# A decoder's MLP in eight blocks of 512 inner features, its second product as seven block products summed in DRAM

## The chip, the cores and the metric

The kernel runs on one core of a Trainium2 chip. Such a core has TensorE (PE, with its weight loads PEld), VectorE (DVE), ScalarE (ACT), GpSimd (POOL), SyncE (SP, which here only issues DMAs) and 16 DMA engines. Each engine works through its own queue in order and waits on semaphores for the others. The metric is device time in microseconds of one execution; the median of several runs counts.

## The reference

Two layers of a hybrid decoder on 512 tokens with 1024 features, then a last RMS norm. In each layer a wide projection feeds sliding-window attention and a retention branch, which are gated and added (that half is not touched here), and then comes the MLP:

```
x = x + mixed @ w_out
h2 = rmsnorm(x, g_mlp)
x = x + jnp.square(jax.nn.relu(h2 @ w_up)) @ w_down     # w_up 1024 x 4096, w_down 4096 x 1024
...
return rmsnorm(x, g_final)                               # after both layers
```

Everything is float32. The kernel gets its accuracy from three products of rounded parts: each operand is split into hi (rounded by ScalarE to the matmul's type) and lo (the rest, by VectorE), and hi·hi + hi·lo + lo·hi are summed in PSUM.

## The kernel before

x lies transposed in SBUF: features in partitions (8 chunks of 128), the 512 tokens in columns. A matmul has a 128x128 block of a weight as its stationary operand and 512 (or 256) tokens as the moving one, and its output has features in partitions again.

**Weights** come in units of 128x1024 (512 KB) in one order fixed beforehand (`unit_order`). `load_until` issues the loads on SP's queue into a ring of three raw buffers, `split_until` has ScalarE write hi (L235) and VectorE lo (L236) into rings of three each, and `unit` hands the next pair to the products and asks for the splits up to three units further on. `products` (L280 to L282) issues the three matmuls of each 128x128 block.

**First product of the MLP.** The first 512 inner features are a plain product (`group`, four units, four PSUM banks, `put_up`). The other 3584 come in 14 pairs of two 128-feature chunks (`pair`): a product of two by two blocks made with seven block products in place of eight. For it the weights are added to each other (`load_part`, `add_part`, VectorE), the input's four sums are made once per layer (`sum_input`), PSUM results are copied or added by ScalarE and VectorE (L1037 to L1049), each block product has 256 tokens, 12 matmuls, and relu, the RMS factor and the square follow (L1053, L1054, L1057). The result is split into hi and lo and kept in slots (`Slots`: nine tiles of 128x2048, given out in quarters or whole).

**Second product.** The inner features are taken in four quarters of 1024. `mlp_sequence` writes the order out by hand: the pairs of the next quarter alternate with `two_chunks` of w_down for the quarter before (two output chunks, two units, 48 matmuls of 512 tokens), whose result VectorE adds to x (L1064). The last quarter comes after all pairs: in layer 0 a group of four chunks and four single ones, and as each chunk of x is done the next layer's input is scaled, split, squared and spilled. In layer 1 `end` takes the tokens in two halves of 256, so that the last norm of the first half goes on beside the second half's products; it squares, sums over features with a matmul against ones, takes the root and reciprocal, multiplies and stores.

All instructions are ordered by a scheduler from the order in which the program issues them; on one engine they then run in that order.

Of the kernel before, what the change touches and what calls it, by code (L numbers as in the profile page):

```python
# [17 lines left out]
P = 128  # L18
# [25 lines left out]
N_IN = 46  # L44
UNIT = 1024
# [3 lines left out]
DELAY = 2  # L49


def unit_order():
# [9 lines left out]
    for what, q, i in mlp_sequence():  # L62
        if what == "first":
            order += [("w_up", u) for u in range(4)]
        elif what == "pair":
            order += [("pair", 8 * q + 2 * i, part) for part in range(4)]
        elif what == "down":
            order += [("w_down", 8 * q + 2 * i + u) for u in range(2)]
        else:
            order += [("w_down", 8 * q + u) for u in range(8)]  # L70
    return order


def mlp_sequence():

    seq = [("first", 0, 0), ("pair", 0, 2), ("pair", 0, 3)]
    for q in range(3):
        for i in range(4):  # L80
            seq += [("down", q, i), ("pair", q + 1, i)]
    return seq + [("last", 3, 0)]
# [32 lines left out]
def decoder(ctx, tc, xT, x_first, w_in, w_a, w_b, w_out, w_up, w_down, tables, decay, band, out):  # L115
# [14 lines left out]
    def temp(name="t"):  # L130
        return tmp.tile([P, T], F32, tag="t", name=name)
# [23 lines left out]
    raws, parts, homes = {}, {}, []  # L155
# [6 lines left out]
    def raw_tile():  # L162
        return wpool.tile([P, UNIT], F32, tag="raw", name="raw")

# [7 lines left out]
    def load_until(n):  # L172
        while state["loaded"] < min(n, len(order)):
            i = state["loaded"]
            layer, name, j = order[i][:3]
            if name == "pair":
                load_part(i)
            else:
# [13 lines left out]
    def load_part(i):  # L192
        layer, _, j, part = order[i]
        if part == 0:
            raws[i] = raw_tile()
            nc.sync.dma_start(raws[i][:, LEFT], w_up[layer, j][:, LEFT])
            raws[i + 3] = raw_tile()
            nc.sync.dma_start(raws[i + 3], w_up[layer, j + 1])
        elif part == 1:
            raws[i] = big("raw2").rearrange("p a t -> p (a t)")  # L200
            nc.sync.dma_start(raws[i][:, RIGHT], w_up[layer, j][:, RIGHT])

    def add_part(i):
        part = order[i][3]
        if part == 0:
            w2 = raws[i + 3]
            nc.vector.tensor_tensor(raws[i][:, RIGHT], w2[:, RIGHT], w2[:, LEFT], ALU.add)
        elif part == 1:
            w1 = raws[i - 1]
            nc.vector.tensor_tensor(raws[i][:, LEFT], w1[:, RIGHT], w1[:, LEFT], ALU.subtract)  # L210
        elif part == 2:
            raws[i] = big("raw3").rearrange("p a t -> p (a t)")
            w1, w2, z2 = raws[i - 2], raws[i + 1], raws[i - 1]
            nc.vector.tensor_tensor(raws[i][:, LEFT], w1[:, LEFT], w2[:, RIGHT], ALU.subtract)
            nc.vector.tensor_tensor(raws[i][:, RIGHT], z2[:, RIGHT], z2[:, LEFT], ALU.subtract)

    def split_until(n):
        while state["split"] < min(n, len(order)):
            i = state["split"]
            load_until(i + 3)  # L220
            paired = order[i][1] == "pair"
            if paired:
                add_part(i)
            raw = raws[i]
            if homes and i >= len(order) - len(homes):
                home = homes[len(order) - 1 - i]
                hi, lo = (home[:, 2 * a : 2 * a + 2, :].rearrange("p a t -> p (a t)") for a in range(2))
            else:
                hi = wpool.tile([P, UNIT], F32R, tag="hi", name="hi")
                lo = wpool.tile([P, UNIT], F32R, tag="lo", name="lo")  # L230
# [172 lines left out]
    def end(layer, uT):  # L403
# [5 lines left out]
        def unit_at(i):  # L409
            if len(units) == i:  # L410
                units.append(unit("w_down", layer))
            return units[i]
# [841 lines left out]
```

## Time and profile before

| | |
|---|---|
| median of 3 runs | 1511.3 us (1511.27 to 1512.82) |
| the profiled execution | span 1511.4 us, 20498 instructions |
| PE busy | 99%, 8080 matmuls |
| VectorE, ScalarE, POOL busy | 68%, 49%, 0% |
| HBM read, written | 146.96 MB, 4.19 MB |
| MLP of layer 0, of layer 1 (from the timeline) | about 415 to 753 us, 1160 to 1501 us |

The page has one row for each group of equal instructions: line, engine, operation, output and inputs by the program's names, shapes and count, then busy time and mean of one in ns, then the idle time ahead of them and what ended it. A wait row has engine, line, "<-" what it waited for, total us, times and the longest. A timeline row has start and duration in us.

### The profile page before, as it was taken

Reading aid. Unit: us, or ns where it says so; the run is one execution under the profiler, and the core shown is the slowest. Engines: PE = TensorE matmul, PEld = TensorE weight load, DVE = VectorE, ACT = ScalarE, POOL = GpSimd, SP = SyncE. Lnnn points to the kernel's source line nnn. Section 1 sums busy time; section 2 is a strip of 40 time slices with the busy share of each in tenths; the row PEclk is TensorE's granted clock in tenths of the full one; section 3 lists DMA queues with packets and bytes.
Section 4 is the critical chain, followed back from the end, with each engine's and each line's share of the span. In section 5 each row is a group of like instructions: output and inputs, shape, how many; then the busy total and the mean of one; then the engine's idle time right before and its main releaser. Section 6 shows DMA issues by size and latency. Waiting matters only on the chain.

```text
span 1511.4 us, 20498 instructions
## 1 busy us (share of the span) xinstructions
PE 1499.2 (99%) x8080; PEld 1302.2 (86%) x8080; DVE 1026.7 (68%) x1598; ACT 740.1 (49%) x1163; POOL 2.9 (0%) x13
## 2 busy tenths in 40 slices
PE   9999999999999999999999999999999999999997
PEld 7888888888888999989888888888888999889997
DVE  6877668754787666676678765777449866666664
ACT  6656455632564444444455742555327544444452
POOL 0000000000000000000000000000000000000000
PEclk9999999999999999999999999999999999999999
DMA  6422322233223232233442222222342232232331
GB/s 217 123 97 75 98 79 91 70 125 126 98 78 104 98 112 97 93 104 115 165 131 93 84 84 98 82 79 84 126 125 98 85 104 92 99 111 98 103 108 56
DMA packets 52640, 155.10 MB, mean 103 GB/s; under 512 B 6208, under 2 KB 8384, under 8 KB 52544
## 3 DMA queue, kind: packets, MB, share of 16 engines
q1 hardware_dynamic: 52400, 153.54, 30.6%
q8 instruction: 63, 1.03, 0.3%
q14 instruction: 33, 0.27, 0.1%
q10 hardware_dynamic: 144, 0.26, 0.0%
HBM read 146.96 MB, written 4.19 MB: 100 GB/s over the span
## 4 chain that ended last, share of the span: by engine, by line
PE 98%; ACT 1%; DVE 0%; DMA 0%; issue 0%; DVEq 0%
PE mm L280 29%; PE mm L281 29%; PE mm L282 29%; PE rv L280 2%; PE rv L281 2%; PE rv L282 2%; PE score L651 1%; PE pT L616 1%; PE r L281 1%; PE r L282 1%; PE r L280 1%; PE pv L637 0%; PE pv L636 0%; PE ssq L374 0%; PE ret L281 0%; PE ret L282 0%
## 5 line engine op out<-in xcount | busy, mean ns | idle before, releaser
L235 ACT ACTIVATE hi<-raw 128x1024 fp32r<-128x1024 f32 (+1 forms) x313 | 314.6, 1013 | 517.9 <-PE mm L281 430.6
L236 DVE TENSOR_TENSOR lo<-raw,hi 128x1024 fp32r<-128x1024 f32 (+1 forms) x314 | 362.6, 1164 | 162.0 <-ACT hi L235 161.1
L281 PE MATMUL mm<-r,hi 128*128 128x512 f32 (+1 forms) x1136 | 392.5, 346 | 0.0
L280 PE MATMUL mm<-r,hi 128*128 128x512 f32 (+1 forms) x1136 | 389.5, 346 | 1.0 <-ACT mm L1037 1.0
L282 PE MATMUL mm<-r,lo 128*128 128x512 f32 (+1 forms) x1136 | 388.5, 346 | 0.0
L280 PE MATMUL mm<-xh,hi 128*128 128x512 f32 (+1 forms) x1008 | 358.2, 357 | 0.9 <-ACT xh L290 0.9
L281 PE MATMUL mm<-xl,hi 128*128 128x512 f32 (+1 forms) x1008 | 356.8, 356 | 0.0
L282 PE MATMUL mm<-xh,lo 128*128 128x512 f32 (+1 forms) x1008 | 355.4, 356 | 0.0
L280 PEld LDWEIGHTS mm<-r,hi 128*128 128x128 f32 x1136 | 214.8, 189 | 27.8 <-ACT mm L1037 1.4
L281 PEld LDWEIGHTS mm<-r,hi 128*128 128x128 f32 x1136 | 215.3, 189 | 26.3
L282 PEld LDWEIGHTS mm<-r,lo 128*128 128x128 f32 x1136 | 215.0, 189 | 25.7
L280 PEld LDWEIGHTS mm<-xh,hi 128*128 128x128 f32 x1008 | 191.1, 190 | 27.1 <-ACT xh L290 1.6
L281 PEld LDWEIGHTS mm<-xl,hi 128*128 128x128 f32 x1008 | 191.3, 190 | 25.5
L282 PEld LDWEIGHTS mm<-xh,lo 128*128 128x128 f32 x1008 | 191.0, 190 | 25.5
L1064 DVE TENSOR_TENSOR x<-x,mm 128x512 f32<-128x512 f32 x56 | 37.8, 687 | 34.2 <-PE mm L282 34.2
L282 PE MATMUL rv<-hi,xl 128*128 128x512 f32 x128 | 49.8, 389 | 0.0
L281 PE MATMUL rv<-lo,xh 128*128 128x512 f32 x128 | 49.8, 389 | 0.0
L280 PE MATMUL rv<-hi,xh 128*128 128x512 f32 x128 | 49.4, 391 | 0.0
L281 PE MATMUL mm<-ulo,hi 128*128 128x512 f32 (+1 forms) x128 | 46.3, 363 | 0.0
L280 PE MATMUL mm<-uhi,hi 128*128 128x512 f32 (+1 forms) x128 | 46.2, 362 | 0.0
L282 PE MATMUL mm<-uhi,lo 128*128 128x512 f32 (+1 forms) x128 | 45.7, 365 | 0.0
L1044 DVE SCALAR_TENSOR_TENSOR z<-mm,rstd 128x256 f32<-128x256 f32 x28 | 11.9, 425 | 42.0 <-PE mm L282 42.0
(188 smaller groups left out, 1682.1 us busy)
## 6 DMA issues: line engine op xcount, KB each, us to landing
raw<-w_in_in SPq DMA_DIRECT2D x89, 512.0 KB, 3.3
raw<-w_down_in SPq DMA_DIRECT2D x64, 512.0 KB, 3.3
raw<-w_up_in SPq DMA_DIRECT2D x36, 512.0 KB, 3.3
raw<-w_up_in SPq DMA_DIRECT2D x56, 256.0 KB, 2.7
raw<-w_b_in SPq DMA_DIRECT2D x16, 512.0 KB, 3.2
raw<-w_out_in SPq DMA_DIRECT2D x16, 512.0 KB, 3.5
raw<-w_a_in SPq DMA_DIRECT2D x8, 512.0 KB, 3.3
x<-xT_in SPq DMA_DIRECT2D x15, 256.0 KB, 3.6
```

What stands on the lines that cost most here:

```text
L235: nc.scalar.activation(hi[:, at], raw[:, at], AF.Copy)
L236: nc.vector.tensor_tensor(lo[:, at], raw[:, at], f32(hi[:, at]), ALU.subtract)
L280: nc.tensor.matmul(ps, ah, bh, start=start and i == 0, stop=False, **more)
L281: nc.tensor.matmul(ps, ah, bl, start=False, stop=False, **more)
L282: nc.tensor.matmul(ps, al, bh, start=False, stop=stop and i == n - 1, **more)
L616: nc.tensor.transpose(pt[:, i * P : (i + 1) * P], sm[:, at : at + P], ident)
L651: nc.tensor.matmul(ps[:, g * w : (g + 1) * w], q_s[g][:, c, at], part[:, keys], start=i == 0, stop=i == 1)
L1044: nc.vector.scalar_tensor_tensor(z[:, 0, :H], a, 0.0, rms_mlp.value[:, :H], ALU.max, ALU.mult)
L1064: nc.vector.tensor_tensor(x[:, c, :], x[:, c, :], ps, ALU.add)
```

## The change

The MLP of a layer becomes eight blocks of 512 inner features. A block is its first product (the group for block 0, two pairs for the others) and then, at once, its second product `down(e)`. No quarter is delayed any more; `mlp_sequence` is gone.

`down(e)` multiplies a block's 512 tokens x 512 inner features by 512 x 1024 of w_down as two by two blocks with seven block products. The operands change places: the activations are the stationary operand, 128 tokens each, and the split weights are the moving one, 512 output features wide. The output thus has tokens in partitions. A block product is 2 token chunks x 2 inner chunks x 3 = 12 matmuls of 512 columns. The activations' sums are made by `Forms`, the weights' sums by VectorE (`add_block`) or by an adding DMA on POOL's queue (`load_block`: a plain load on SP's queue, then `accum_op` add on top). w_up's sums, too, come partly from adding DMAs now (`load_part`), and raw weights have six buffers and no use of the big ones.

Each block's four quarters of y (tokens x features) are copied or added out of PSUM into a temporary (`Adding.put`) and added by DMA on POOL's queue into a DRAM buffer y. The RMS factor, which before went into each relu, now goes in once at the end as its square (`column_factors`, per token in partitions). In the last block `Ending` loads y, adds the quarters to it with the factor and, in layer 0, turns the result by PE into x (`turn`), then scales, splits, squares and spills it; the last part of that is done within the next layer's first group (`carry`). In layer 1 x is turned instead (`add_x`), and squares, root and the last gain are per token; the output leaves with tokens in partitions.

```
+AHEAD = 5
-            load_until(i + 3)
+            load_until(i + AHEAD)
...
+        return wpool.tile([P, UNIT], F32, tag="raw", name="raw", bufs=6)
+        return tmp.tile([P, T], F32, tag="t", name=name, bufs=7)
...
+    def load_block(i):
+        layer, _, j, part = order[i]
+        b11, b12, b21, b22 = (w_down[layer, j + a] for a in range(4))
+        if part in (2, 5):
+            return
+        raws[i] = raw = raw_tile()
+        nc.sync.dma_start(raw, {0: b11, 1: b21, 3: b12, 4: b11, 6: b22}[part])
+        if part in (1, 4):
+            nc.gpsimd.dma_start(raw, b22 if part == 1 else b21, accum_op=ALU.add)
+
+    def add_block(i):
+        part = order[i][3]
+        if part in (2, 5):
+            base, other = (i - 2, i - 1) if part == 2 else (i - 3, i - 2)
+            raws[i] = raws.pop(base)
+            nc.vector.tensor_tensor(raws[i], raws[i], raws.pop(other), ALU.add)
...
+        def keep_up(z):
+            nc.scalar.activation(z, z, AF.Square)
+            if not kept:
+                split(first_hi, first_lo, z[:, :, :H])
+                u_forms.one(0, z)
+                u_forms.keep(0, 0, u_forms.f[0], (0,))
+                kept.append(z)
+            else:
+                u_forms.rest(0, kept.pop(), z, (1,))
+                split(u_two[:, 0:2, :], u_two[:, 2:4, :], z)
...
+        def down(e):
+            def multiply(ps, moving, start=True):
+                hi, lo = unit("block", layer)
+                for m in range(2):
+                    at = slice(m * P, (m + 1) * P)
+                    pairs = []
+                    for k, (uh, ul) in enumerate(moving):
+                        cols = slice(k * T, (k + 1) * T)
+                        pairs.append(((uh[:, at], ul[:, at]), (hi[:, cols], lo[:, cols])))
+                    products(ps[m], pairs, start, True, not start)
...
+            multiply(a, b11)
+            for m in range(2):
+                nc.scalar.activation(b[m], a[m], AF.Copy)
+            multiply(c, u_forms[0])
+            for m in range(2):
+                nc.scalar.activation(p5[m], c[m], AF.Copy)
+            multiply(b, u_forms[1], False)
+            for m in range(2):
+                nc.scalar.activation(u2[m], b[m], AF.Copy)
+            sink.begin(0)
+            multiply(a, b21, False)
+            for m in range(2):
+                sink.put(0, 0, m, a[m], 1)
+            sink.begin(1)
+            multiply(b, u_forms[2], False)
+            for m in range(2):
+                sink.put(1, 1, m, b[m], -1, p5[m])
+            sink.begin(2)
+            multiply(c, b22, False)
+            for m in range(2):
+                sink.put(0, 1, m, c[m], 1, u2[m])
+            sink.begin(3)
+            multiply(b, u_forms[3], False)
+            for m in range(2):
+                sink.put(1, 0, m, b[m], -1)
+            sink.begin(4)
+
+        class Adding:
+            def put(self, i, j, m, ps, sign, more=None):
+                t = temp("y")
...
+                how = {"accum_op": ALU.add} if self.e else {}
+                nc.gpsimd.dma_start(y[:, 2 * j + m, i * T : (i + 1) * T], t, **how)
...
+        class Ending:
...
+            def scale_all(self):
+                for i, j in QUADS:
+                    for m in range(2):
+                        v = self.y[i, j, m]
+                        nc.scalar.activation(v, v, AF.Copy, scale=factor[:, 2 * j + m : 2 * j + m + 1])
...
+            def turn(self, i, j):
+                for half in range(2):
+                    ps = bank(ps_mm, "turn")
+                    for k in range(2):
+                        for m in range(2):
+                            v = self.y[i, j, m]
+                            nc.tensor.transpose(
+                                ps[:, (2 * k + m) * P : (2 * k + m + 1) * P],
+                                v[:, (2 * half + k) * P : (2 * half + k + 1) * P],
+                                ident,
+                            )
+                    xa = x[:, 4 * i + 2 * half : 4 * i + 2 * half + 2, j * H : (j + 1) * H]
+                    nc.vector.tensor_tensor(xa, xa, ps.rearrange("p (a t) -> p a t", t=H), ALU.add)
...
+        for e in range(N_BLOCK):
+            if e == 0:
+                group("w_up", layer, xs, [put_up(c) for c in range(4)], first_hooks())
+            else:
+                pair()
+                pair()
+            down(e)
```

More of the change, by code (lines that the diff above doesn't have):

```diff
@@ L44 @@
 N_IN = 46
+N_BLOCK = 8
 UNIT = 1024
@@ L1060, in pair @@
[L1060 to L1070 removed]
+            multiply(b, part, True, sums[3], False)
+            nc.scalar.activation(z[:, 1, :H], b, AF.Relu, scale=-1.0)
```

405 lines of the change are left out of this document (210 added, 195 removed).

## The prediction

> **What bounds the kernel now.** I read the page first, then the waits of PE, the windows of the first layer's MLP, and the timeline there. Page, parts 1 to 4:
>
> ```profile
> PE 1499.2 (99%) x8080; PEld 1302.2 (86%) x8080; DVE 1026.7 (68%) x1598; ACT 740.1 (49%) x1163; POOL 2.9 (0%) x13
> PEclk9999999999999999999999999999999999999999
> q1 hardware_dynamic: 52400, 153.54, 30.6%
> PE 98%; ACT 1%; DVE 0%; DMA 0%; issue 0%; DVEq 0%
> ```
>
> PE is busy all through, its clock never falls, and 98% of the chain that ended last is PE. Its waits, all there are (times, longest):
>
> ```profile
> PE warm L260 <- DVE ones L255: 1.1, 1, 1.1
> PE mm L280 <- ACT mm L1037: 1.0, 2, 0.5
> PE mm L280 <- ACT xh L290: 0.9, 1, 0.9
> PE ssq L439 <- ACT sq L431: 0.5, 1, 0.5
> ```
>
> So a matmul taken away is time taken away, and a wait put in is time put in. Two windows of the MLP (busy us and count of PE, PEld, DVE, ACT, POOL), and its timeline, which gives the step from matmul to matmul:
>
> ```profile
> 520.00:560.00 40.00, 40.00 (x254) 36.39 (x253) 26.37 (x35) 17.47 (x25) 0.00 (x0) 1.00 0.29 101
> 560.00:600.00 40.00, 40.00 (x250) 36.17 (x249) 26.70 (x38) 17.64 (x26) 0.00 (x0) 1.00 0.29 96
> ...
> 605.38 0.39 PE L280 MATMUL mm<-uhi,hi 128*128 128x512 f32 x1
> ...
> 607.65 0.28 PE L280 MATMUL mm<-r,hi 128*128 128x256 f32 x1
> ...
> 608.96 0.28 PE L282 MATMUL mm<-r,lo 128*128 128x256 f32 x1
> ...
> 99.55 0.60 PE L616 MATMUL pT<-ident,sm 128*128 128x128 f32 x4
> 99.91 0.72 PE L651 MATMUL score<-r,r 128*128 128x256 f32 x4
> ```
>
> From 605.38 to 607.65 lie ten matmuls of 512 columns: 0.227 us each (the 0.39 is the time in the pipeline). From 607.65 to 608.96 lie eleven of 256: 0.119. A turn of a 128x128 block costs 0.36/4 = 0.09. VectorE and ScalarE have 34% and 56% of the time free here.
>
> **The matmuls.** Before, w_down takes 32 units of 24 matmuls in a layer: 768 of 512 columns in layer 0; in layer 1 576 of 512 and, in the halves at the end, 384 of 256. After, a block of 512 inner features takes 7 products of 12 matmuls of 512: 8 x 84 = 672 in each layer. w_up keeps its count. Layer 0: -96 x 0.227 = -21.8 us. Layer 1: +96 x 0.227 - 384 x 0.119 = -23.9. Together -45.7 us. Added are 32 turns a layer (x or y between tokens in columns and in partitions): 64 x 0.09 = +5.8. The sums over features change by a dozen small matmuls: 0. The moving operand is now a weight and the stationary one an activation; both pass PE as 512 columns in the values of the retention already, so I keep 0.227.
>
> **What the first product of a block waits for.** Before, a quarter's w_down groups stood between pairs of the next quarter, so that a pair's output had ten microseconds to be squared and split. After, the seven products of block e use the output of the two pairs just ahead of them, and the weights come in a fixed order through three hi and three lo buffers, so nothing later can go ahead. Durations for the chain (ScalarE, then VectorE, by shape; then hand-overs):
>
> ```profile
> L235 ACT ACTIVATE hi<-raw 128x1024 fp32r<-128x1024 f32 x280 | 293.9, 1058 | 497.9 <-PE mm L281 410.6 <-issue 64.4 <-PE rv L282 14.5
> L287 ACT ACTIVATE r<-sums 128x1024 fp32r<-128x1024 f32 x8 | 8.4, 1052 | 0.4 <-DVE sums L991 0.4
> L287 ACT ACTIVATE r<-z 128x512 fp32r<-128x512 f32 x56 | 35.3, 631 | 5.4 <-DVE z L844 4.0
> L822 ACT ACTIVATE rr<-r 128x512 f32<-128x512 f32 x16 | 9.6, 601 | 12.9 <-PE r L282 12.8
> L1042 ACT ACTIVATE eu<-mm 128x256 f32<-128x256 f32 x28 | 10.8, 384 | 16.2 <-PE mm L282 16.2
> ...
> L236 DVE TENSOR_TENSOR lo<-raw,hi 128x1024 fp32r<-128x1024 f32 x280 | 339.9, 1222 | 138.2 <-ACT hi L235 137.3
> L288 DVE TENSOR_TENSOR r<-z,r 128x512 fp32r<-128x512 f32 x56 | 38.0, 685 | 0.7 <-ACT r L287 0.5
> L291 DVE SCALAR_TENSOR_TENSOR r<-rv,rcol,r 128x512 fp32r<-128x512 f32 x16 | 11.3, 745 | 4.2 <-ACT r L290 4.2
> ...
> 1500.82 0.28 PE L282 MATMUL mm<-r,r 128*128 128x256 f32 x1
> 1501.14 0.42 DVE L426 TENSOR_TENSOR x<-x,mm 128x256 f32<-128x256 f32 x1 [1.55 <-PE mm L282]
> 1501.60 0.42 ACT L431 ACTIVATE sq<-x 128x256 f32<-128x256 f32 x1 [1.92 <-DVE x L426]
> ```
>
> An engine starts 0.04 us after the one it waits for. In the order in which the changed kernel's queues are built, PE runs: first product of the block (it needs the first pair alone), last product of the second pair (starts at F), second product (first pair alone), then the product of b21, which needs the second pair's squared output. PE is free for it at F + 12 x 0.119 + 12 x 0.227 = F+4.2. ScalarE's queue up to what it needs: weights of unit 2 until F+1.3, copy of the first product's second bank 0.60, weights of unit 3 (their buffer is free once the pair's last product is done, F+1.6) 1.06, so F+2.9; relu of 256 columns 0.38; square of 128x1024 1.05; the two copies of the second product 1.20, which stand ahead; split of the output 1.05: F+6.7 with six hand-overs 6.9. PE stands 2.7 us. It then has four matmuls (0.9) until it needs the form t2, whose split stands behind the weights of unit 4: 6.9 + 1.06 + 0.63 = F+8.6, so 0.8 more. A block of this kind costs **3.5 us of wait, where its matmuls save 12 x 0.227 = 2.7**. Seven such blocks a layer: 14 x 3.5 = 49. The first block of a layer comes from the group instead: by the same steps (relu twice, square, weights, split before its first product) 2.3 + 0.4 + 0.5 = 3.2; two: 6.4. Bounds for a block: 0.8, if the copies and weights ahead cost nothing, and 6, if each piece that stands ahead comes in full on top.
>
> **Other work.** A block gives ScalarE 17 pieces of 1024 columns, 17 of 512 and 8 of 256 (17.9 + 10.4 + 3.0 = 31.3 us) and VectorE 17, 17 and 4 (20.8 + 11.7 + 1.7 = 34.2), beside PE's 84 x 0.227 + 168 x 0.119 = 39.1. Both hold, with little spare: what is late stays late.
>
> **The DMAs.**
>
> ```profile
> raw<-w_down_in SPq DMA_DIRECT2D x64, 512.0 KB, 3.3
> raw<-w_up_in SPq DMA_DIRECT2D x56, 256.0 KB, 2.7
> raw<-w_in_in SPq DMA_DIRECT2D x5, 256.0 KB, 5.8
> y_out<-o SPq DMA_DIRECT2D x4, 256.0 KB, 2.2
> ```
>
> A block moves 5.24 MB by SP's queue (2 x 1280 KB for the pairs, 5 x 512 for w_down) and 4.19 MB by POOL's with an add (4 x 256 and 2 x 512 KB of weights, 8 x 256 of y). No row shows an adding DMA. The queue's 153.54 MB took 30.6% of 1511.4 us, so full would be 332 GB/s: 15.8 us plain and 12.6 for the adding ones if they cost like plain ones, 28.4 of 42.6. Latency of one: between 2.2 (a plain store) and 5.8 (a load while the DMAs are full). Most loads start 7 us or more before they are split. The tightest is the next pair's first unit: its buffer is free at F-7.1, the load lands at F-3.8, the add at F-1.6 to F+2.0; VectorE comes to it at F+0.6, ahead of its own pieces of the chain above. Late by 1.4 us it costs 0.9 a block (the second half of the output's split), so 0 to 13 us in all; I take 0, since 256 KB loads in mid-kernel take 2.7. On POOL's queue these weights stand ahead of the block's own y, and an add that waits holds them; their buffers (seven for fourteen uses a block) are wanted again half a block, 20 us, later, so that is hidden unless adds take several times as long.
> A rule bears on this. The Trainium skill, "Collectives: The Full Stack", section "The bandwidth ceiling: the fold count and why AG ≠ RS ≠ AR", says that a reducing DMA is half as fast because it reads two sources. By it a block's DMAs would take 15.8 + 25.2 = 41.0 of 42.6 us, and the sum would stay as it is but with 4% to spare, which speaks for the second rival below; no run here shows it yet.
>
> **The two ends of the MLP.** Layer 0's last block scales y (8 x 0.60 on ScalarE, ahead of weights: 1 us), adds each quarter into it, turns it, adds it to x and splits x before the next layer's first matmul. After the b22 product VectorE has some ten pieces of 0.7 and ScalarE one, against 2.7 us of PE: 5 us. Together +6 (3 if only the last pieces show, 12 if all do). The last block of layer 1 gives VectorE twenty pieces of 0.745 (eight for the turned x, twelve for the quarters) in place of four, +12 us in 24: it ends some 3 us after PE. Then:
>
> ```profile
> L375 ACT ACT_TABLE_LOAD x8 | 10.3, 1283 | 2.8 <-PE ssq L374 2.7
> ...
> 1505.10 2.77 DVE L467 TENSOR_TENSOR o<-x,rstd 128x256 f32<-128x256 f32 x8
> 1507.70 0.93 SPq L469 DMA_DIRECT2D y_out<-o  x2
> ```
>
> Before, from the last product's end (1501.1) to the end is 10.3 us. After: two adds 1.5, square 0.8, table 1.3, root and reciprocal 0.4, eight products 6.0, small ones 0.8, the store and its landing 3.2: 14. So +4, with VectorE's lag +7 (2 to 12).
>
> **Sum**, against the profiled execution, whose span of 1511.4 us is the median's 1511.3: -45.7 + 5.8 + 49 + 6.4 + 6 + 7, and -1.5 for the MLP's own two waits that go: +27, **1538 us**. Own range 1515 to 1560 (stalls of 2.2 to 4.5 a block with the bounds of the ends).
>
> **Rivals.** (1) Faster. ScalarE reaches the relu as soon as the pair is done, with neither the weights of unit 3 (1.06) nor the second product's copies (1.20) and their hand-overs ahead: the output's split is then done at F+4.2, when PE comes, and 2.5 of the 3.5 us are gone. 1538 - 16 x 2.5 = 1498. For it: ScalarE is idle half the time now. Against it: the queue is in order and the weights wait for the same product as the relu. It is faster than before once the wait is under 1.8 us a block. (2) The adding DMAs become the bound. From 2.1 times a plain one on, 15.8 + 12.6 x 2.1 = 42.3, a block lasts as long as its DMAs; at 2.5 times 47.3, that is 4.7 x 14 = +66: 1604; at 3 times 53.6: 1692. For it: nothing shows what an adding DMA costs. Against it: 30.6% now. The skill's two reads stand just under the point from which it decides. (3) Waits and savings cancel within what a measurement can tell, 0.2% (3 us): 1511.
>
> **How the numbers follow.** Forecast 0.54, rival 1 0.20, rival 2 0.22, rival 3 0.04. Range 1490 to 1640: below it are waits under 0.8 a block, above it adds of over 2.7 times, together under 0.2. Faster 0.20, same 0.04, slower 0.76 (forecast and rival 2).
>
> **What would show it.** PE should lose some 60 us of idle time: in each block about 2.7 us ahead of the b21 product, released by ScalarE's split of the squared output, and 0.8 ahead of the third product; PE's matmuls fall by 318, the step stays 0.227, the clock stays full. ScalarE's and VectorE's share in the MLP should rise to about 75 and 80%. Right on DMAs is: POOL's queue under 35% of the engines in the MLP, no PE wait that leads to raw. It is wrong if PE's waits lead to raw and DMA shares near 100%, if the clock falls in the waits, or if no wait stands ahead of b21.

## The result and the profile after

The changed kernel takes **1642.95 us** (median of 4, 1632.39 to 1645.09), the kernel before 1511.28 (4 runs, 1510.63 to 1512.82): ratio 1.0855, 95% interval 1.0823 to 1.0888. That is 132 us more, where the prediction had 27 more and a range that ended at 1640. The profiled execution has a span of 1642.4 us.

The page of the changed kernel, its lines on the engines, the clock, the DMAs, their queues and the chain that ended last (by engine, then by line):

```profile
PE 1514.1 (92%) x7766; PEld 1278.1 (78%) x7766; DVE 1105.3 (67%) x1622; ACT 902.0 (55%) x1429; POOL 173.6 (11%) x213
...
PEclk9999999999999999999999999999999899998998
DMA  6421322343379767887843223223444697777974
...
q1 hardware_dynamic: 59392, 172.94, 32.0%
q0 software_dynamic: 27776, 60.83, 21.0%
...
PE 63%; DMA 20%; DVE 8%; issue 6%; ACT 3%; DVEq 0%; POOL 0%; POOLq 0%; ACTq 0%
DMA raw<-w_up_in 19%; PE mm L284 16%; PE mm L283 16%; PE mm L282 16%; DVE lo L237 4%; PE rv L282 2%; PE rv L283 2%; PE rv L284 2%; PE b L284 1%; ACT hi L236 1%; PE b L283 1%; PE b L282 1%; DVE r L290 1%; PE score L620 1%; PE pT L585 1%
```

PE has 314 matmuls less (318 by the forecast), and yet 63% of the chain in place of 98%; 20% of it are DMAs, 19% the loads of w_up and the adding DMAs on top of them. The two MLPs stand out in the DMA row (6 to 9 tenths). q0 is POOL's queue with the adding DMAs: 60.83 MB in 21.0% of 1642.4 us is 176 GB/s if it ran alone, where q1 (172.94 MB in 32.0%) makes 329.

The waits of PE in the changed kernel (us in all, times, longest):

```profile
PE mm L283 <- DVE lo L237: 39.3, 15, 5.9
PE mm L282 <- ACT r L289: 31.3, 16, 2.8
PE mm L282 <- ACT eu L1019: 19.9, 12, 3.4
PE mm L284 <- DVE lo L237: 9.6, 10, 2.9
```

The second line is the wait that was forecast, ahead of the b21 product. The first was not: PE waits for the low half of a split weight, up to 5.9 us. Who is late is to be seen in VectorE's timeline of one block (in brackets the idle time ahead and what ended it):

```profile
531.79 1.23 DVE L218 TENSOR_TENSOR raw<-raw 128x1024 f32<-128x1024 f32 x1 [3.57 <-DMA raw<-w_down_in]
...
538.89 0.69 DVE L201 TENSOR_TENSOR raw<-raw 128x512 f32<-128x512 f32 x1 [4.74 <-DMA raw<-w_up_in]
539.50 1.22 DVE L237 TENSOR_TENSOR lo<-raw,hi 128x1024 fp32r<-128x1024 f32 x1
...
541.90 1.22 DVE L237 TENSOR_TENSOR lo<-raw,hi 128x1024 fp32r<-128x1024 f32 x1
543.03 0.68 DVE L391 SCALAR_TENSOR_TENSOR sums<-sums,z 128x512 f32<-128x512 f32 x1
...
544.24 0.68 DVE L201 TENSOR_TENSOR raw<-raw 128x512 f32<-128x512 f32 x1
544.84 0.69 DVE L394 SCALAR_TENSOR_TENSOR sums<-sums,z 128x512 f32<-128x512 f32 x1
```

L201 is the add of w_up for the **next** block's first pair. It stands in VectorE's queue ahead of two splits of w_down (539.50, 541.90) and of the sums t2 to t4 (L391 to L394) that the **current** block's products need, and waits 4.74 us for an adding DMA. Nothing behind it can go. The DMA is late for a reason that its own chain shows; the pieces of the chain that ended last, in order of time:

```profile
524.25 9.68 DMA raw<-w_up_in
...
534.60 4.21 DMA raw<-w_up_in
...
538.89 0.10 DVE raw L201
```

A plain load (9.68 us, issued behind five loads of w_down), then an adding DMA on top of it (4.21), then the add: 14.6 us in series from the moment the raw buffer is free. Other blocks show the same chain: at 472, 680 and 1290 us the load takes 8.88, 9.70 and 10.36 us and the adding DMA 4.0. What PE makes of it, by its timeline:

```profile
543.17 0.80 PE L283 MATMUL mm<-lo,r 128*128 128x512 f32 x1 [3.06 <-DVE lo L237]
543.76 0.63 PE L282 MATMUL mm<-hi,r 128*128 128x512 f32 x1
544.19 0.63 PE L283 MATMUL mm<-lo,r 128*128 128x512 f32 x1
...
548.68 0.39 PE L283 MATMUL mm<-lo,r 128*128 128x512 f32 x1
548.91 0.40 PE L284 MATMUL mm<-hi,r 128*128 128x512 f32 x1
```

After the waits a matmul of 512 columns takes a step of 0.43 us (543.76 to 544.19), by 548.68 it is 0.23 again: these waits cost more than their length. The granted clock is 0.50 from 543.7 to 547.7. The Trainium skill, "TensorE: Matmul & The Clock Gate", section "What's actually happening", says that the clock is gated by how busy PE has been lately; the half rate behind the waits agrees with it. Two windows of 26 us, the first with these waits, the second behind it, and the two stretches of the chain's load and adding DMA (last three columns: granted clock, share of the DMA engines, GB/s):

```profile
524.00:550.00 26.00, 17.96 (x80) 13.55 (x81) 16.99 (x21) 13.93 (x22) 3.07 (x4) 0.87 0.57 128
550.00:576.00 26.00, 25.43 (x173) 23.41 (x172) 13.85 (x17) 13.78 (x23) 8.82 (x10) 1.00 0.96 228
524.00:534.00 10.00, 8.26 (x50) 6.84 (x50) 6.24 (x9) 5.12 (x11) 1.35 (x2) 1.00 0.93 216
534.00:539.00 5.00, 2.56 (x10) 1.80 (x10) 0.26 (x2) 4.97 (x8) 0.86 (x1) 1.00 0.52 107
```

Over the first window no engine is full, and the DMA engines are at 0.57. That speaks against a plain lack of DMA throughput, and for a chain. Yet the 0.57 is a mean: the load's 9.68 us fall where the engines are at 0.93, the adding DMA's 4.21 where they are at 0.52. So the longest link of the chain is long where the engines are nearly full. From block to block (ScalarE's copy of the first product, read off its timeline) the second to seventh steps of layer 0 take 54.5, 51.8, 53.0, 49.7, 52.0 and 51.5 us. I use the mean of these twelve steps of both layers below: 51.7 here. The forecast had 39.1 + 3.5 = 42.6.

### The profile page after: what moved, and what is told of

Same layout as the page of the kernel before. It is cut to its first block, busy times and chain, and to the rows that moved or that the text cites. A ratio compares the mean times of both kernels' runs of the same rounds, so it can differ in the third digit from the quotient of the medians.

```text
span 1642.4 us, 21085 instructions
## 1 busy us (share of the span) xinstructions
PE 1514.1 (92%) x7766; PEld 1278.1 (78%) x7766; DVE 1105.3 (67%) x1622; ACT 902.0 (55%) x1429; POOL 173.6 (11%) x213
## 3 DMA queue, kind: packets, MB, share of 16 engines
q1 hardware_dynamic: 59392, 172.94, 32.0%
q0 software_dynamic: 27776, 60.83, 21.0%
## 4 chain that ended last, share of the span: by engine, by line
PE 63%; DMA 20%; DVE 8%; issue 6%; ACT 3%; DVEq 0%; POOL 0%; POOLq 0%; ACTq 0%
DMA raw<-w_up_in 19%; PE mm L284 16%; PE mm L283 16%; PE mm L282 16%; DVE lo L237 4%; PE rv L282 2%; PE rv L283 2%; PE rv L284 2%; PE b L284 1%; ACT hi L236 1%; PE b L283 1%; PE b L282 1%; DVE r L290 1%; PE score L620 1%; PE pT L585 1%
## 5 line engine op out<-in xcount | busy, mean ns | idle before, releaser
L236 ACT ACTIVATE hi<-raw 128x1024 fp32r<-128x1024 f32 (+1 forms) x366 | 373.0, 1019 | 457.1 <-PE mm L283 221.8
L237 DVE TENSOR_TENSOR lo<-raw,hi 128x1024 fp32r<-128x1024 f32 (+1 forms) x367 | 427.0, 1171 | 194.8 <-ACT hi L236 189.3
L282 PE MATMUL mm<-r,hi 128*128 128x256 f32 (+1 forms) x768 | 253.4, 330 | 2.5 <-ACT mm L1017 2.5
L283 PE MATMUL mm<-r,hi 128*128 128x256 f32 (+1 forms) x768 | 252.7, 329 | 0.0
L284 PE MATMUL mm<-r,lo 128*128 128x256 f32 (+1 forms) x768 | 252.7, 329 | 0.0
L282 PEld LDWEIGHTS mm<-r,hi 128*128 128x128 f32 x768 | 147.4, 192 | 17.0 <-ACT mm L1017 3.9
L283 PEld LDWEIGHTS mm<-r,hi 128*128 128x128 f32 x768 | 147.4, 192 | 13.0
L284 PEld LDWEIGHTS mm<-r,lo 128*128 128x128 f32 x768 | 147.5, 192 | 12.3
L283 PE MATMUL mm<-lo,r 128*128 128x512 f32 x256 | 110.4, 431 | 39.3 <-DVE lo L237 39.3
L282 PE MATMUL mm<-hi,r 128*128 128x512 f32 x256 | 100.4, 421 | 33.5 <-ACT r L289 31.3
L1102 POOL DMA_DIRECT2D y<-y x112 | 103.1, 1012 | 97.3 <-ACT y L1096 69.4
L284 PE MATMUL mm<-hi,r 128*128 128x512 f32 x256 | 103.1, 415 | 3.5 <-DVE r L290 3.3
L201 DVE TENSOR_TENSOR raw<-raw 128x512 f32<-128x512 f32 x56 | 38.6, 690 | 95.3 <-DMA raw<-w_up_in 86.9
L283 PEld LDWEIGHTS mm<-lo,r 128*128 128x128 f32 x256 | 52.1, 204 | 58.9 <-DVE lo L237 48.4
```

The lines of the kernel that those rows point to most:

```text
L201: nc.vector.tensor_tensor(raws[i][:, at], last[:, LEFT], last[:, RIGHT], ALU.add)
L236: nc.scalar.activation(hi[:, at], raw[:, at], AF.Copy)
L237: nc.vector.tensor_tensor(lo[:, at], raw[:, at], f32(hi[:, at]), ALU.subtract)
L282: nc.tensor.matmul(ps, ah, bh, start=start and i == 0, stop=False, **more)
L283: nc.tensor.matmul(ps, ah, bl, start=False, stop=False, **more)
L284: nc.tensor.matmul(ps, al, bh, start=False, stop=stop and i == n - 1, **more)
```

## The experiments

All against the kernel before in the same session (1511 to 1513 us). "Block" is that mean step.

| run | what differs from the changed kernel | us | ratio, 95% interval | block |
|---|---|---|---|---|
| changed | | 1642.95 | 1.0855 (1.0823 to 1.0888) | 51.7 |
| e1 | no adding DMAs | 1532.9 | 1.0141 (1.0126 to 1.0156) | 42.7 |
| e2 | weights' adds go aside | 1574.0 | 1.0412 (1.0396 to 1.0427) | 43.8 |
| e3 | all adds made plain stores | 1560.4 | 1.0317 (1.0297 to 1.0337) | 45.4 |
| e4 | 7 raw buffers, 6 temporaries | 1657.6 | 1.0961 (1.0942 to 1.0980) | 52.0 |
| e5 | no y adds | 1593.0 | 1.0539 (1.0504 to 1.0574) | 47.3 |
| e6 | w_up's sums on VectorE | 1595.9 | 1.0544 (1.0523 to 1.0565) | 47.7 |
| e7 | all weights' sums on VectorE | 1588.9 | 1.0514 (1.0493 to 1.0534) | 46.9 |
| e8 | e7, forms made earlier | 1594.9 | 1.0552 (1.0530 to 1.0574) | 47.2 |
| e9 | four own tiles for y | 1674.7 | 1.1078 (1.1044 to 1.1112) | 54.3 |
| e10 | e9 with 7 raw buffers | 1721.0 | 1.1391 (1.1372 to 1.1410) | 57.4 |
| e11 | e5 with 7 raw buffers | 1623.1 | 1.0737 (1.0713 to 1.0761) | 49.1 |
| e12 | e1, forms made earlier | 1517.6 | 1.0036 (1.0025 to 1.0047) | 41.0 |
| e13 | L201 moved behind the forms | 1585.9 | 1.0489 (1.0467 to 1.0511) | 46.2 |
| e14 | e13, b21+b22 on VectorE | 1601.9 | 1.0593 (1.0570 to 1.0616) | 48.1 |
| e15 | e14, forms made earlier | 1584.3 | 1.0478 (1.0462 to 1.0494) | 46.4 |
| e16 | e13 with all sums on VectorE, forms earlier | 1590.2 | 1.0517 (1.0490 to 1.0543) | 46.8 |
| e17 | e13 without y's adds | 1538.7 | 1.0173 (1.0143 to 1.0202) | 42.9 |
| e18 | e13, forms made earlier | 1563.4 | 1.0343 (1.0326 to 1.0360) | 44.4 |

### Is it the adding DMAs at all, and is it their throughput? (e1 to e4)

**e1** takes all adding DMAs out:

```
-            nc.gpsimd.dma_start(raw[:, RIGHT], two[1][:, LEFT], accum_op=ALU.add)
-            nc.gpsimd.dma_start(raw[:, LEFT], two[0][:, RIGHT], accum_op=ALU.add)
-        if part in (1, 4):
-            nc.gpsimd.dma_start(raw, b22 if part == 1 else b21, accum_op=ALU.add)
...
-                nc.gpsimd.dma_start(y[:, 2 * j + m, i * T : (i + 1) * T], t, **how)
+                if self.e == 0:
+                    nc.gpsimd.dma_start(y[:, 2 * j + m, i * T : (i + 1) * T], t)
```

> Left out: all adding DMAs (of w_up, of w_down, and y of the blocks after the first, which is then simply not stored), so the weights of six forms are wrong and y is that of the first block alone; all loads by SP, all splits, all matmuls stay. What is left is my forecast's own chain (ScalarE ahead of the b21 product, ends of the layers). Theory A (the loss beyond the forecast comes from the adding DMAs, by whatever way): the forecast's sum holds, 1538 us (1515 to 1560), PE waits for raw tiles near zero, clock 1.00. Theory B (it comes from somewhere else, such as the fuller queues of ScalarE and VectorE): 1600 or more.

Measured 1532.9. PE's waits and a window of one block (columns as above):

```profile
PE mm L278 <- ACT r L285: 27.0, 16, 1.9
PE b L278 <- ACT r L285: 3.5, 13, 0.3
```

```profile
524.00:566.00 42.00, 39.98 (x254) 35.56 (x253) 32.26 (x39) 29.18 (x45) 0.00 (x0) 1.00 0.39 126
```

Theory A holds: the fuller queues of ScalarE and VectorE cost what the forecast's block costs (42.7 for 42.6), and the other 110 us come with the adding DMAs.

**e2** sends the adds of weights to tiles in DRAM that nobody reads:

```
-            nc.gpsimd.dma_start(raw[:, RIGHT], two[1][:, LEFT], accum_op=ALU.add)
+            add_aside(two[1][:, LEFT])
```

> The adding DMAs of weights (four a block on w_up, two on w_down) keep their source, size and place in POOL's queue, but add into tiles in DRAM that nobody reads, so no raw tile waits for them; the weights of six forms are wrong. Adding y stays. Bytes moved and added are those of the changed kernel. Theory C (a serial chain: raw buffer free, load, add, VectorE, split, next buffer; latency): 1540 to 1565 us. Theory D (the DMA engines' time: an adding byte takes 1.9 times a plain one, 40 of a block's 42.6 us): 1620 to 1645, as the engines have the same to do.

1574.0, but the run did not do what it was for. With nothing to wait for, the adds were put at the front of POOL's queue. The first of them that adds and the last in POOL's timeline, and a window there beside one in the MLP:

```profile
9.47 0.87 POOL L193 DMA_DIRECT2D aside<-w_down_in  x1 [4.54 <-DMA aside<-w_down_in]
...
239.26 0.81 POOL L193 DMA_DIRECT2D aside<-w_up_in  x1 [2.58 <-DMA aside<-w_up_in]
```

```profile
0.00:40.00 40.00, 28.77 (x91) 21.14 (x92) 19.46 (x27) 17.77 (x28) 13.99 (x28) 0.89 1.01 277
```

```profile
520.00:560.00 40.00, 37.14 (x242) 33.47 (x240) 28.98 (x35) 27.52 (x43) 7.04 (x8) 1.00 0.70 185
```

They filled the DMA engines (1.01) for the first 240 us and delayed the first MLP by some 30 us (its first copy at 471.8, in the changed kernel at 440.0). What can be read from it is the MLP, which has y's adding DMAs alone: a block of 43.8, only 1.1 us above none.

**e3** makes every adding DMA a plain store of the same bytes in the same place:

```
-                how = {"accum_op": ALU.add} if self.e else {}
+                how = {}
```

(and the same for the three lines of the weights).

> All adding DMAs stay in place, on POOL's queue, with their bytes and their waits, but store instead of adding (sums of weights and y are wrong). Tells the price of the add from the price of a second DMA in the chain. Theory D: a block's DMAs fall from 40 to 28 us of engine time, and 1540 to 1560 us come back. Theory C: the chain keeps its links and each adding one becomes shorter by the add alone (8 to some 5 us, 5 to 4), about 2 us on each of the two to four links a block: 1575 to 1605.

1560.4, at the upper end of theory D's range and 15 us below theory C's: 83 of the 110 us go with the add. Its queue row, against the one of the changed kernel above:

```profile
q0 software_dynamic: 18048, 60.83, 11.0%
```

The same bytes in 11.0% of 1564.8 us are 353 GB/s, for 176 with the add. So adding about halves the rate. Both rows hold 4.2 MB of plain stores (the first blocks' y, 0.7% of 1532.8 us in e1); without them the adding DMAs make 170 GB/s, so an added byte costs 2.1 times a plain one of this queue and 1.95 times one at the 332 of the forecast. The Trainium skill, "Collectives: The Full Stack", section "The bandwidth ceiling: the fold count and why AG ≠ RS ≠ AR", gives a half for the reduce step of a collective, whose add reads two sources; the factor measured here, outside a collective, agrees. Yet 45.4 us a block is still 2.7 above none: the second DMA in the chain costs without the add too.

**e4** gives the ring of raw tiles a seventh buffer, with the room of one temporary:

```
-        return wpool.tile([P, UNIT], F32, tag="raw", name="raw", bufs=6)
+        return wpool.tile([P, UNIT], F32, tag="raw", name="raw", bufs=7)
```

(AHEAD 6 for 5; the ring "t" 6 for 7.)

> Nothing left out. One raw buffer more (7 for 6) and loads one unit further ahead (6 for 5); the ring of temporaries gets 6 in place of 7 to make room. Theory C: each lap of the ring carries one unit more, a block's 12 buffers are 1.7 laps in place of 2, so of the 10 us that a block loses some 4 come back: 1575 to 1610. Theory D: no change, 1635 to 1650.

1657.6, 15 us slower. Neither theory had that. PE's waits for splits of weights were halved (39.3 to 20.3 us), but 20.5 us of waits for VectorE's y came up. I took that for the want of temporaries and tested it with e9.

### Which of the adds, and can VectorE do them? (e5 to e8)

**e5** leaves out y's adds (the last three lines of e1's diff).

> Left out: y of the blocks after the first is not stored (the output lacks their part); the sums of weights are added by POOL's DMAs as in the changed kernel, in their place. A block's DMA time falls from 39.8 (5.24 MB at 329 GB/s, 4.19 MB at 176) to 28 us. Theory C (serial chain of raw buffer, load, adding DMA, VectorE, split): its links stay and shorten only by what they lose in contention: a block of 45 to 49 us for 42.1 without adds, 1575 to 1630 us in all. Theory D (engines' time) and theory E (an adding DMA of weights stands behind y's in POOL's queue): 42 to 43 us a block, 1533 to 1550.

1593.0 and 47.3 us a block: 50 us come from y's adds, and theories D and E fall, since 4.6 us a block stay with the DMA engines at 0.6.

**e6** loads the two halves of w_up plainly and lets VectorE add:

```
+        elif part == 2:
+            nc.sync.dma_start(raw, two[0])
...
+        if order[i][3] == 2:
+            nc.vector.tensor_tensor(raws[i][:, LEFT], raws[i][:, LEFT], raws[i][:, RIGHT], ALU.add)
```

> Nothing left out. The two sums of w_up that POOL's DMAs add are made by VectorE from plainly loaded tiles (four adds of 512 columns more a block, 2.8 us; 1.05 MB that was added is loaded plainly). w_down's two adding DMAs and y's eight a block stay. DMA time of a block: 6.29 MB plain 19.1 us and 3.15 MB added 17.9, together 37.0 for 39.8. Theory C: the chain through raw<-w_up is cut: 1540 to 1565. Theory D: 37.0 for 39.8, 7% less: 1600 to 1635.

1595.9: 47 us back, half of what theory C asked, and 4 us below D's range.

**e7** does the same for w_down, with a second tile:

```
+            raws[i, 1] = other = big("wb").rearrange("p a t -> p (a t)")
+            nc.sync.dma_start(other, b22 if part == 1 else b21)
...
+            nc.vector.tensor_tensor(raws[i], raws[i], raws.pop((i, 1)), ALU.add)
```

> Nothing left out. As the one before, and the two sums of w_down are made by VectorE too, from a second tile loaded plainly (two adds of 1024 columns, 2.4 us a block); only y is still added by DMA. DMA time 7.34 MB plain 22.3 and 2.10 MB added 11.9: 34.2 us of a block. Both C and D give back the loss: 1533 us plus what 5.2 us a block more on VectorE costs (34.2 becomes 39.4 of 42 us; 0 to 2 us a block): 1535 to 1565. If it stays over 1600, y's adds are the cause.

1588.9, 24 us above its range. No weight is added by DMA any more, and 4.2 us a block stay. The waits of VectorE and ScalarE in e7:

```profile
ACT y L1101 <- DMA y<-y: 43.7, 18, 4.1
DVE raw L197 <- DMA raw<-w_up_in: 38.3, 16, 3.7
DVE raw L219 <- DMA wb<-w_down_in: 36.3, 18, 5.3
```

VectorE waits for plain loads as it did for adding ones, mostly at the sums of the second pair (L197) and of w_down (L219). What of it reaches PE no run here separates.

**e8** is e7 with the second half of the pair's output squared, and its forms made, before the pair's last product:

```
             nc.scalar.activation(z[:, :, H:], z[:, :, H:], AF.Relu)
+            nc.scalar.activation(z[:, :, H:], z[:, :, H:], AF.Square)
+            if kept:
+                u_forms.before(0, kept[0], z)
```

> Nothing left out. As the one before, and the wait that my forecast placed ahead of the b21 product is shortened: the second half of the second pair's output is squared, and the forms that need it alone are made and split, before the pair's last product; only the first half is squared after it. In the run without adds that wait was 27.0 us over 16 blocks. If it is ScalarE's queue, as forecast, 15 to 27 us less than the kernel before this one: 1510 to 1545. If the wait only moves to the next piece, no change.

1594.9: nothing gained. PE's wait ahead of the b21 product fell from 27.6 to 6.7 us, and 23.8 us of waits for VectorE's splits came in its place.

### Depth or order? (e9 to e12)

**e9** gives y four tiles of its own, **e10** is e9 with e4's edit, **e11** is e5 with e4's edit. e9:

```
+        stage = ninth(F32)
+        staged = [stage[:, i, :] for i in range(4)]
...
-                t = temp("y")
+                t = staged[0]
+                staged.append(staged.pop(0))
```

> Nothing left out. The pieces of y that wait for their adding DMAs get four tiles of their own (one of the nine r tiles, which is free during the MLP), and the ring of seven temporaries is left to the pair and product copies. Theory F (y's adds, 8 us each and held up in POOL's queue behind adds of weights that wait 5 to 11 us for their load, keep the temporaries, and ScalarE and VectorE wait for these): the 27.8 us of ScalarE waiting for y's DMA and the 20 us of PE waiting for the copies eu go: 1600 to 1625 us. Theory C (chain of raw tiles alone): 1635 to 1645.

> Nothing left out. The same four tiles for y, and the seventh raw buffer with loads one unit further ahead, as in the run before that took its room from the temporaries and got no faster. If that run gained on the raw tiles (PE waiting for splits of weights fell from 39 to 20 us in it) what it lost on the temporaries (20 us of new waits for y), theory C with F: 1575 to 1605. If depth does not matter (theory D, engines' time): as the run before this one.

> Left out: y of the blocks after the first, as in the run of 1593 us with adding of weights alone (46.3 us a block, 42.0 without any add). Seven raw buffers for six, loads one unit further ahead. Theory C: one more unit of slack is worth some 3.5 us a block (42 us over 12 units), so most of those 4.3 us go: 1540 to 1565 us. Theory D, or a chain that the depth of the ring does not set: 1585 to 1600.

1674.7, 1721.0 and 1623.1: all three slower, by 32, 78 and (against e5) 30 us. A raw buffer more did not help, against theory C. VectorE's timeline in e11 shows why:

```profile
538.62 1.42 DVE L201 TENSOR_TENSOR raw<-raw 128x512 f32<-128x512 f32 x2 [5.15 <-DMA raw<-w_up_in]
539.95 2.35 DVE L237 TENSOR_TENSOR lo<-raw,hi 128x1024 fp32r<-128x1024 f32 x2
...
543.36 0.68 DVE L391 SCALAR_TENSOR_TENSOR sums<-sums,z 128x512 f32<-128x512 f32 x1
```

With one buffer more, **both** adds of the next pair (x2) stand ahead of this block's splits and sums. In the changed kernel it was one, the other between L393 and L394. Buffers free earlier let the adds be placed earlier in the queue; the DMA they wait for came no earlier (the add starts at 538.62, in the changed kernel at 538.89). e4 and e10 have both adds ahead too. So these runs change the order along with the depth, and depth alone was not tested.

e9 did not test what it was for. Its four tiles are fewer than the seven that y shared with the copies, and the engines wait more for y's DMAs: ScalarE 80.1 us (27.8 in the changed kernel), VectorE 46.1 (4.1). The place of the first pair's adds is that of the changed kernel. So e9 does not refute theory F; in e9 tiles that a late adding DMA holds do cost time.

**e12** is e1 with e8's edit.

> Left out: all adding DMAs, as in the run of 1533 us. The second half of the second pair's output is squared and its forms made ahead of the pair's last product, so that ScalarE has 2 us less to do between that product and the product of b21. If the wait there (27.0 us over 16 blocks) is ScalarE's queue, as I forecast: 1503 to 1518. If it only moves to another piece of the same chain: 1528 to 1535.

1517.6, 15.3 less, at the upper end of the range. PE's waits in e12:

```profile
PE b L280 <- DVE r L286: 12.0, 14, 0.9
...
PE mm L278 <- ACT r L285: 3.8, 2, 1.9
```

The wait ahead of b21 went from 27.0 to 3.8 us, 12.0 of it came back as a wait for the split of t3 or t2. So that wait was ScalarE's queue, as forecast.

### The place in VectorE's queue (e13 to e18)

**e13** changes only where the adds of w_up stand: they multiply by a one that is made of the last split of the current block.

```
+        one = small.tile([P, 1], F32, tag="one", name="one", bufs=2)
+        nc.vector.tensor_scalar(one, src, 0.0, 1.0, ALU.mult, ALU.add)
...
-            nc.vector.tensor_tensor(raws[i][:, at], last[:, LEFT], last[:, RIGHT], ALU.add)
...
+                nc.vector.scalar_tensor_tensor(
+                    raws[i][:, at], last[:, LEFT], behind[0], last[:, RIGHT], ALU.mult, ALU.add
+                )
...
+                stay_behind(f32(u_forms.tiles[0][1][1][:, 3, 0:1]))
```

> Nothing left out, all adding DMAs as in the changed kernel. Only the place of VectorE's adds of w_up in its queue changes: they multiply by a one that is made from the last split of the current block's forms, so they stand behind it and no longer ahead of the split of w_down's second sum and of the sums of the block's output. Theory G (the late adding DMA costs because VectorE waits for it in order, with this block's work behind): the waits of VectorE at these adds (86.9 us in all, 4.7 in the traced block) no longer reach PE: 1560 to 1600 us. Theory C (the weights come too late for PE itself): the wait moves to the split of the pair's weights: 1620 to 1650.

1585.9: **57 us back**, with all DMAs in place. VectorE's timeline and PE's waits in e13:

```profile
580.07 0.69 DVE L403 SCALAR_TENSOR_TENSOR sums<-sums,z 128x512 f32<-128x512 f32 x1
580.67 0.69 DVE L405 TENSOR_TENSOR sums<-z 128x512 f32<-128x512 f32 x1
581.27 0.69 DVE L406 SCALAR_TENSOR_TENSOR sums<-sums,z 128x512 f32<-128x512 f32 x1
...
586.00 0.15 DVE L201 TENSOR_SCALAR one<-r 128x1 f32<-128x1 f32 x1
586.19 1.54 DVE L209 SCALAR_TENSOR_TENSOR raw<-raw,one 128x512 f32<-128x512 f32 x2
```

```profile
PE mm L294 <- ACT r L301: 30.2, 16, 2.9
PE mm L294 <- ACT eu L1032: 17.4, 10, 3.0
PE mm L296 <- DVE lo L249: 8.8, 11, 1.2
...
PE mm L295 <- DVE lo L249: 1.6, 3, 0.6
```

The sums come one after another and the adds (L209) behind them, with no wait. Of VectorE's 86.9 us of waits at these adds in the changed kernel, 53.1 (in nine blocks) stood at the first pair's, ahead of work that was ready, and 33.8 at the second pair's. In e13 the first are gone in every block and 30.0 are left, all at the second pair's. PE's waits for splits of weights, 39.3 and 9.6 us in the changed kernel, are 1.6 and 8.8 here, and the forecast's wait is the largest.

**e14** is e13 with e7's way for b21 + b22 alone, **e15** is e14 with e8's edit, **e16** is e13's edit on e8. e14:

```
-        if part in (1, 4):
-            nc.gpsimd.dma_start(raw, b22 if part == 1 else b21, accum_op=ALU.add)
+        if part == 1:
+            raws[i, 1] = other = big("wb").rearrange("p a t -> p (a t)")
+            nc.sync.dma_start(other, b22)
+        if part == 4:
+            nc.gpsimd.dma_start(raw, b21, accum_op=ALU.add)
```

> Nothing left out. As the run before, and the first of w_down's two sums (b21 + b22, which the second and third product need) is made by VectorE from two plainly loaded tiles in place of a load with an adding DMA behind it; the other add of w_down, those of w_up and y's stay. ScalarE waited 4.9 and VectorE 3.6 us for that add in the traced block, but only some of it reaches PE (25 + 12 us of waits by the trace): 15 to 35 us less than the run before, 1535 to 1580. If its lateness does not count: 0 to +15 (VectorE has 1.2 us a block more).

> Nothing left out. As the run before, with the second half of the pair's output squared and its forms made before the pair's last product, which was worth 15.3 us without the adding DMAs and nothing with all sums on VectorE. If the adding DMAs no longer stall VectorE: 10 to 16 us less than the run before. If another wait for them takes its place: no change.

> Nothing left out. All sums of weights on VectorE (the run that took 1594.9 us), with the adds of w_up behind the current block's last split. Theory G: those adds wait for plain loads now (38 us of waits in that run) and stand in the same place of the queue: moved behind, 20 to 50 us come back: 1545 to 1575. If VectorE's load (5.2 us a block more) is what costs there: 1585 to 1600.

e14: 1601.9, 16 us slower than e13. The add was brought into VectorE's queue, and there it waits; the wait and the landing in e14:

```profile
DVE raw L231 <- DMA wb<-w_down_in: 68.5, 14, 6.7
```

```profile
wb<-w_down_in SPq DMA_DIRECT2D x16, 512.0 KB, 9.4
```

That is the same mistake once more, with a plain load of 9.4 us in place of an adding DMA. e15: 1584.3, 18 less than e14. e16: 1590.2, where its place in the queue was to give 1575 at most; against e8, which has the same sums on VectorE and the same edit, the moved adds gave 4.7 us, within the two intervals. But they were not the adds that wait: e13's edit holds back the two adds of a pair that it held back there, and in e8 these wait for no DMA. The two sums that e7 gave to VectorE stay where they were, and e16 still waits 41.2 us at one of them (L204, nearly all at the second pair) and 39.4 at w_down's (L231). So e16 does not tell these waits from VectorE's greater load (the other theory's 1585 to 1600).

**e17** is e13 without y's adds, **e18** is e13 with e8's edit.

> Left out: y of the blocks after the first is not stored, as in the run of 1593 us. VectorE's adds of w_up stand behind the block's forms, as in the run of 1585.9. If the two causes are apart and add up (50 us for y's adds, 57 for the place in the queue): 1535 to 1550. If y's adds cost only by making the adding DMAs of weights later, they cost less now: 1555 to 1580.

> Nothing left out. Moved adds of w_up, and the second half of the pair's output squared and its forms made ahead of the pair's last product. PE waited 30.2 us over 16 blocks for the split of the squared output in the run with the moved adds. If that wait stands by itself: 1565 to 1576. If the late weights in ScalarE's queue take its place: 1580 to 1590.

e17: 1538.7. With the changed kernel, e5 and e13 this is a table of two by two: y's adds away 50 us, adds moved 57, both 104. They add up within 3 us, and what is left is e1 (1532.9) and 6 us. The greatest wait of PE in e17 is the forecast's own:

```profile
PE mm L294 <- ACT r L301: 29.2, 16, 2.8
```

e18: 1563.4, 22 less than e13 and the fastest here of those that leave nothing out; it remains 3.4% slower than the kernel before.

**What stays open**: by which way y's adds cost 47 us (e13 against e17). A window of e17 has the DMA engines at 0.66, one of e18, with y's adds, at 0.91; in e2, where y's adds have POOL's queue to themselves in the MLP, they cost 1.1 us a block. So there they cost beside the weights' adds, not alone. The waits narrow it down. ScalarE waits 44.0 us for weights of w_up in e13 and 4.3 in e17, and 34.3 and 2.1 us for y's DMAs; behind the late weights stand copies (eu) for which PE waits 17.4 us in e13 and not at all in e17. In one such block of e13 (1425 to 1442 us) the profile has the DMA engines at 1.07 to 1.10. So y's adds make the next weights late. How much of that is the full engines and how much POOL's one queue was not told apart.

## Why the prediction was wrong, by its steps

**The step that failed** is in "The DMAs": the next pair's first unit, "I take 0". The place was right (VectorE comes to it "ahead of its own pieces of the chain above"), and so was the way, but the price was made with a load of 3.3 us and an add of 2.2 to 5.8. In the traced block the add took 4.21 us, within its bounds, but the load took 9.68 behind five loads of w_down, with the DMA engines at 0.93. VectorE stood 4.74 us, where I had 1.4, and the stall ran through the whole queue behind it: 57 us in all (e13), where my upper bound was 13. I priced what the late add itself holds back ("the second half of the output's split"), not the two splits of w_down and the three sums that stood behind it.

**A second step failed**: y's adds, "hidden unless adds take several times as long", cost 47 to 50 us (e13 against e17, changed against e5). An add landed after 8.1 us where a plain store took 4.5 (e3):

```profile
y<-y POOLq DMA_DIRECT2D x112, 256.0 KB, 8.1
```

These two terms are 104 of the 110 us between e1 and the changed kernel.

**Rival 2** had the right suspect with the wrong way. By the 332 GB/s of the forecast an adding DMA costs 1.95 times a plain one, under the 2.1 from which it was to decide: 15.8 + 12.6 x 1.95 = 40 of 51.7 us. The block lasted as long as a chain, and e13 took 5.5 us off it with every byte in place. But the price of the add is in the chain: 83 us go in e3, where the same DMAs store, and it is while the engines are at 0.93 that the load takes 9.68 us. In e18, at 44.4 us a block, the 40 are not far.

**The b21 wait** was right in place and cause: 31.3 us in 16 blocks, up to 2.8 for the 2.7 forecast, released by ScalarE's split, and e12 takes it away by making that queue shorter. The idle time in e1 is smaller, up to 1.9 + 0.3 for 3.5, yet a block has 42.7 us for the 42.6 of the forecast. That agreement is partly luck. Seven of the twelve steps take 42.0 to 42.1 us, which leaves 40.0 for the matmuls where the forecast had 39.1. The other five take 43.3 to 44.0: there the same waits are followed by some 3 us of matmuls at 0.43 us a step (571.3 to 574.7), and the granted clock of such a block is 0.96 in place of 1.00.

**The sum without the DMA terms** came out: 1538, e1 1532.9, in part by errors that cancel. The ends were oversized (in e1 PE waits 2.2 us at the hand-over between the layers for the 6 of the forecast). Wrong as well: "the clock stays full"; that it falls in the waits was one of the prediction's own signs of being wrong. The granted clock was 0.968 in the changed kernel and 0.87 in the window above.

**Rival 1** (faster) fell in all runs; the nearest to it, e12, is 0.4% slower than before, and leaves the adding DMAs out.

## What to carry to other kernels

Price a late transfer by the whole queue of the engine that waits for it, not by the piece that needs it: look up what stands behind that wait in the order in which the queue was built, and whose work it is. A load followed by an adding DMA is two latencies in series, and the load must be taken from where the DMA engines are busy (9.7 us here), not from a quiet stretch (3.3). More buffers can change the order: where a scheduler fills the queues, they can move a waiting instruction ahead of work that was ready (e4, e10, e11), and one false dependency that holds it back (e13) was worth 57 us.

## What the runs showed that I had not expected

- An adding DMA moves bytes at half the rate of a plain one on the same queue, and the target makes no difference. Without the 4.2 MB of plain stores POOL's queue makes 170 GB/s in e5, where it adds into SBUF alone (35.66 MB in 12.3% of 1593.1 us), and 170 in e7, where it adds into DRAM alone (29.37 MB in 10.0% of 1588.0); plain it makes 353 (e3).
- Waits of 2.8 and 3.1 us (at 539.6 and 543.2 in the traced block) cost PE more than their length: from 543.76 to 547.7 a step of 512 columns took 0.43 us for 0.23, some 2 us more. In e1 waits of 1.75 and 0.27 us (at 569.5 and 570.9) were followed by 3 us of it; so they were in five of twelve blocks, and in the other seven the same waits were not.
- One raw buffer more made the kernel 15 to 46 us slower in three pairs (changed to e4, e9 to e10, e5 to e11; each with one temporary less and loads one unit further ahead).
